# First loads split over two queues, angles started from the second: the opening of a fused pooling and attention layer

## The chip, the cores and the metric

The kernel runs on one core of one Trainium2 chip. The metric is the device time of one execution in microseconds; the median of several executions counts.

## The reference, cut to what matters

One layer on x of 256 tokens by 1024 channels, all in float32: one projection gives six parts, a pooling branch and an attention branch are computed from them, each is multiplied by SiLU of its gate, one output projection follows, then a residual and a layer norm.

```python
proj = jnp.einsum('bsd,de->bse', h, w_in[layer])
u_pool, g_pool, q, k, v, g_attn = jnp.split(proj, cuts, axis=-1)
y_pool = multiscale_pool(u_pool, pool_w[layer], pool_scale[layer]) * jax.nn.silu(g_pool)
q = partial_rotary(q.reshape(b, s, N_HEADS, HEAD_DIM), positions)
k = partial_rotary(k.reshape(b, s, N_HEADS, HEAD_DIM), positions)
y_attn = moba_attention(q, k, v) * jax.nn.silu(g_attn)
out = jnp.einsum('bse,ed->bsd', jnp.concatenate([y_pool, y_attn], axis=-1), w_out[layer])
h = layer_norm(ALPHA * h + out, ln_gain[layer], ln_bias[layer])

def partial_rotary(x, positions):        # the angles that this change moves
    ang = positions.astype(jnp.float32)[..., None] * freqs
    cos, sin = jnp.cos(ang)[:, :, None, :], jnp.sin(ang)[:, :, None, :]
    ...
```

With 256 tokens there is one key block, so attention is causal attention over all keys.

## The kernel before, in words

Every float32 matmul is done as three fast ones: an operand is split into a high part (a cast to fp32r, `hi`, line 307) and a low part (what the cast lost, a subtraction, `lo`, line 318), and high x high, low x high and high x low are added up in PSUM. ScalarE makes the casts (its rows have line 310), VectorE or GpSimd the subtractions (line 320).

The first stage is the value projection v (lines 430 to 462). The inner dimension of 1024 is cut into eight blocks k = 0 to 7 of 128. A block is one row of `xw`: 256 columns of x, transposed, and 512 columns of value weights, 384 KB together. `load_xw` (line 325) loads it, block 0 in two pieces (512 columns, then 256), the others in one. ScalarE casts x and the weights of a block; of block 0 the weights are cast by VectorE in two halves (line 312). VectorE subtracts. TensorE then runs six matmuls of 512 columns a block (line 454; eight in block 0, where the first two are halved): high x times high weights, low x times high weights, high x times low weights.

Behind it come twenty units of 128 output columns, in the order u0 u1 q0 k0 q1 k1 and so on. A unit has its own 512 KB of weights: one load (`load_w`, line 331), one cast by ScalarE, one or two subtractions, 24 matmuls of 256 columns (lines 501 to 503, in two halves of twelve). Rotary embedding (`rope`), scores, softmax, the pooling windows and the gates are interleaved, then the output projection (lines 770 to 772) and the norm follow.

The angles of the rotary embedding have a path of their own. The positions and a small tensor of constants are loaded (`posi`, line 337, and `cst`, line 338). GpSimd multiplies them and reduces the angles to the range of the sine in a chain of small instructions (lines 348 to 377). ScalarE takes two sines (lines 388 and 389), GpSimd makes the cosines (lines 394 and 395), TensorE transposes both (line 526), and ScalarE copies them out (line 529) for `rope`.

TensorE begins with warm-up matmuls on a constant (`warm`, line 297), ScalarE with the load of its function table (line 288).

The order of the instructions on each engine is no list in the source. `add` collects operations with costs by engine; `Plan.run` simulates them, picks on every engine the operation that can start first (among equals the one that is due first), and emits the code in the order of the simulated starts. A constant in the plan can therefore move instructions. Loads are emitted by the plan's engine "SP" whichever queue they go to. A load needs a free slot of `raw` (seven of them), given back by the subtraction that reads it.

Of the kernel before, what the change touches and what calls it, by code (L numbers as in the profile page):

```python
# [63 lines left out]
class Op:  # L64
    __slots__ = ("i", "options", "emit", "bufs", "deps", "outs", "late", "left", "ready", "start", "end", "eng", "pos", "port")


class Plan:
# [4 lines left out]
    MARGIN = 1.0  # L73

# [3 lines left out]
    def add(self, options, emit, reads=(), writes=(), pos=None, port=False):  # L78
        op = Op()
        op.port = port  # L80
# [24 lines left out]
    def run(self, pools, limits, dma_rate=0.34, ahead=3):  # L105
# [5 lines left out]
        for op in reversed(ops):  # L111
            cost = min(c for c in op.options.values())
# [27 lines left out]
        while n < len(ops):  # L140
            best = None
            for e in free:
# [19 lines left out]
                elif e == "SP":  # L162
                    at, op = min(cand, key=lambda c: (c[1].late, c[1].i))
# [58 lines left out]
def hymba_kernel(ctx: ExitStack, tc: tile.TileContext, xw, xn, pos, small_in, w, wo, pw, ln, out):  # L222
# [42 lines left out]
    cst = const.tile([P, RD + 4 + 4 * PAD], F32, name="cst")  # L265
    frq = cst[:, :RD]
    pscale = cst[:, RD:RD + 4]
    fac = cst[:, RD + 4:].rearrange("p (g t) -> p g t", g=4)
    posi = const.tile([P, 2], I32, name="posi")
# [18 lines left out]
    act.preload_act_table_set("trig_and_small")  # L288
# [12 lines left out]
    add({"PE": 3.0}, warm, writes=[wb], pos=at())  # L301


    def load(dst, src, mb, writes):
        add({"SP": mb}, lambda e: nc.sync.dma_start(dst(), src), writes=writes)  # L305

    def hi(dst, src, n, reads, writes, fast=False):
# [5 lines left out]
        options = c_act(n)  # L313
        if fast:
            options["DVE"] = 0.18 + n * 0.00055
        add(options, emit, reads, writes)
# [31 lines left out]
    tiny(lambda e: pool.tensor_copy(posf, posi), ["posi"], ["posf"])  # L348
# [30 lines left out]
    add({"POOL": 3.5}, reduction, [("ang", 0), ("ang", 1)], ["ang"], port=None)  # L379
# [51 lines left out]
    for k in range(KT):  # L431
# [7 lines left out]
        if k == 0:  # L439
            for h in range(2):  # L440
                hi(lambda wH=wH, c=c, h=h: wH[:, c + h * S:c + h * S + S], lambda r=r, h=h: r[:, S + h * S:2 * S + h * S],
                   S, [(r, 1 + h)], [kh(u, k, h)], fast=True)
# [454 lines left out]
```

## Time and profile before

| | us |
|---|---|
| median of 3 runs | 118.07 (117.93 to 118.69) |
| the profiled execution | 118.58 |
| its span in the profile | 116.8 |
| TensorE busy in the span | 108.7 |
| VectorE, ScalarE, GpSimd busy | 81.7, 66.7, 45.8 |

The profile is one execution. Its times start at the first instruction of the span; 1.78 us of the execution lie around the span. PE is TensorE's matmuls, PEld its weight loads, DVE VectorE, ACT ScalarE, POOL GpSimd, SP SyncE; a q behind a name is the engine's sequencer, which issues DMAs and waits. The starts of matmuls are measured, their ends are modelled: a matmul shows longer than it keeps the next one away.

### The profile page before, as it was taken

The page shows a single profiled execution, that of the slowest core. Times are in us where ns is not written, and L with a number is a line of the kernel's source. Part 1 is how long each engine was busy: PE and PEld are TensorE (multiplying, and loading weights), DVE is VectorE, ACT ScalarE, POOL GpSimd, SP SyncE. Part 2 cuts the span into 40 slices and gives each one's busy share as a digit, 9 for nine tenths or more (in the row PEclk, how much of TensorE's full clock was granted, in tenths as well). Part 3 has the DMA queues.
Part 4 walks back from the last instruction along what each step waited for, and adds up shares of the span by engine and source line. Part 5 has one row for each costly group of instructions (what it writes and reads, how often), then busy time and mean ns, then how long its engine had stood idle before and what let it go on. Part 6 is the DMA issues. An engine that isn't in the chain of part 4 may idle for free.

```text
span 116.8 us, 2214 instructions
## 1 busy us (share of the span) xinstructions
PE 108.7 (93%) x809; PEld 98.6 (84%) x809; DVE 81.7 (70%) x182; ACT 66.7 (57%) x132; POOL 45.8 (39%) x66
## 2 busy tenths in 40 slices
PE   7998999999999999999999999999999999999800
PEld 5745889999998999988999898899998989789700
DVE  0539972189999987987868576498897933942780
ACT  4149770599837698598888665524669800120510
POOL 7200687500192689979777320000612600053000
PEclk9999999999999999999999999999999999999997
DMA  3999999929999894596757082500000000022013
GB/s 112 285 349 371 392 384 415 384 108 269 323 316 349 282 349 187 126 412 279 236 205 268 17 264 95 180 6 0 0 0 0 3 6 0 0 90 90 0 54 128
DMA packets 6779, 21.42 MB, mean 183 GB/s; under 512 B 1008, under 2 KB 1520, under 8 KB 6512
## 3 DMA queue, kind: packets, MB, share of 16 engines
q1 hardware_dynamic: 6624, 21.08, 50.7%
q10 hardware_dynamic: 144, 0.20, 0.5%
q8 instruction: 6, 0.10, 0.3%
q14 instruction: 5, 0.04, 0.1%
HBM read 20.23 MB, written 1.05 MB: 182 GB/s over the span
## 4 chain that ended last, share of the span: by engine, by line
PE 60%; DVE 10%; POOL 7%; issue 6%; DMA 6%; ACT 4%; SPq 3%; DVEq 0%; ACTq 0%
PE acc L501 12%; PE acc L502 11%; PE acc L503 11%; DMA posi<-pos 6%; DVE w L320 4%; SPq L305 3%; PE acc L771 3%; PE acc L772 3%; PE acc L770 3%; PE sc L554 3%; PE tp L589 3%; PE sc L771 2%; PE sc L772 2%; PE sc L770 2%; POOL tb L357 2%
## 5 line engine op out<-in xcount | busy, mean ns | idle before, releaser
L501 PE MATMUL acc<-big,w 128*128 128x256 f32 x160 | 45.8, 286 | 0.0
L503 PE MATMUL acc<-big,w 128*128 128x256 f32 x160 | 44.9, 281 | 0.0
L502 PE MATMUL acc<-big,w 128*128 128x256 f32 x160 | 44.8, 280 | 0.0
L320 DVE TENSOR_TENSOR w<-raw,w 128x1024 fp32r<-128x1024 f32 (+1 forms) x31 | 31.2, 1024 | 12.9 <-ACT w L310 11.3
L501 PEld LDWEIGHTS acc<-big,w 128*128 128x128 f32 x160 | 30.2, 189 | 0.7 <-issue 0.5
L502 PEld LDWEIGHTS acc<-big,w 128*128 128x128 f32 x160 | 30.2, 188 | 0.0
L503 PEld LDWEIGHTS acc<-big,w 128*128 128x128 f32 x160 | 30.1, 188 | 0.1
L310 ACT CAST w<-raw 128x1024 fp32r<-128x1024 f32 (+1 forms) x27 | 24.8, 941 | 6.9 <-DMA raw<-xw 3.7
L320 POOL TENSOR_TENSOR w<-raw,w 128x1024 fp32r<-128x1024 f32 x5 | 13.1, 2618 | 12.0 <-ACT w L310 12.0
L454 PE MATMUL acc<-w,big 128*128 128x512 f32 (+1 forms) x50 | 13.4, 419 | 0.8 <-ACT big L310 0.7
L454 PEld LDWEIGHTS acc<-w,big 128*128 128x128 f32 x50 | 9.6, 210 | 4.4 <-ACT big L310 1.9
L579 POOL TENSOR_SCALAR pr<-pr,rv 128x256 f32<-128x256 f32 (+1 forms) x16 | 10.6, 680 | 3.1 <-DVE rv L576 3.1
L475 ACT ACTIVATE w<-raw 128x1024 fp32r<-128x1024 f32 x6 | 6.4, 1061 | 6.9 <-issue 5.0
L320 POOL TENSOR_TENSOR mL<-m,mH 128x256 fp32r<-128x256 f32 x2 | 1.7, 871 | 16.9 <-ACT mH L310 16.9
L573 ACT ACTIVATE pr<-ms,mx 128x256 f32<-128x256 f32 (+1 forms) x16 | 7.1, 448 | 1.1 <-DVE mx L568 1.0
L807 POOL TENSOR_TENSOR xnat<-xnat,gb 128x512 f32<-128x512 f32 x2 | 2.6, 1288 | 11.1 <-ACT xnat L805 11.1
L771 PE MATMUL acc<-w,mH 128*128 128x256 f32 (+1 forms) x18 | 5.7, 319 | 0.0
L772 PE MATMUL acc<-w,mL 128*128 128x256 f32 (+1 forms) x18 | 5.7, 319 | 0.0
L770 PE MATMUL acc<-w,mH 128*128 128x256 f32 (+1 forms) x18 | 5.7, 318 | 0.0
L568 DVE CUSTOM_DVE_ANT_0 ms<-sc,mask 128x256 f32<-128x256 f32 (+1 forms) x16 | 4.8, 347 | 0.8 <-PE sc L554 0.8
L801 ACT ACTIVATE rs<-mv,epst 128x1 f32<-128x1 f32 x1 | 0.3, 295 | 8.5 <-DVE mv L800 8.5
L538 DVE TENSOR_TENSOR qk<-t,t 128x512 f32<-128x512 f32 x4 | 5.1, 1270 | 0.0
(153 smaller groups left out, 195.2 us busy)
## 6 DMA issues: line engine op xcount, KB each, us to landing
raw<-w SPq DMA_DIRECT2D x20, 512.0 KB, 5.4
raw<-wo SPq DMA_DIRECT2D x8, 512.0 KB, 3.5
raw<-xw SPq DMA_DIRECT2D x7, 384.0 KB, 6.7
xnat<-xn SPq DMA_DIRECT2D x1, 1024.0 KB, 7.5
gb<-ln SPq DMA_DIRECT2D x1, 1024.0 KB, 6.2
out<-xnat SPq DMA_DIRECT2D x2, 256.0 KB, 2.0
raw<-xw SPq DMA_DIRECT2D x1, 256.0 KB, 2.7
raw<-pw SPq DMA_DIRECT2D x1, 256.0 KB, 3.3
```

The costliest lines, as they stand in the source:

```text
L310: act.copy(dst(), src())
L320: lambda e: engines[e].tensor_tensor(dst(), raw(), h().bitcast(F32), op=OP.subtract), reads, writes, port=True)
L454: pe.matmul(vb[s][:, o:o + n], x(k, s * P, P), b[:, c + o:c + o + n], start=first and o == 0, stop=last)
L475: act.activation(wH[:, :D], r[:], AF.Identity, accum_out=ws[:])
L501: pe.matmul(o[:, half], wH[:, c], xh(k, 0, S), start=k == 0, stop=False)
L502: pe.matmul(o[:, half], wH[:, c], xl(k, 0, S), start=False, stop=False)
L503: pe.matmul(o[:, half], wL[:, c], xh(k, 0, S), start=False, stop=k == KT - 1)
L573: add(c_act(n, 0.28), lambda e, t=t, sl=sl: act.activation(pr[:, sl], ms[:, sl], AF.Exp, bias=mx[:, t:t + 1], scale=-1.0, accum_out=sm[:, ...
L579: add({"POOL": 0.25 + 0.00105 * n}, lambda e, t=t, sl=sl: pool.tensor_scalar(pr[:, sl], pr[:, sl], rv[:, t:t + 1], 0.5, op0=OP.mult, op1=O ...
L770: pe.matmul(o[:, :n], mH[:, e, sl], wH[:, c0:c0 + n], start=i == 0, stop=False)
L771: pe.matmul(o[:, :n], mH[:, e, sl], wL[:, c0:c0 + n], start=False, stop=False)
L772: pe.matmul(o[:, :n], mL[:, e, sl], wH[:, c0:c0 + n], start=False, stop=i == 7)
```

## The change

Six edits, all at the start of the program:

- Block 0 of x is loaded in other pieces: the 256 columns of x by SyncE's queue, the 512 columns of value weights by ScalarE's queue.
- Positions and constants become one tensor (344 instead of 336 bytes a partition), loaded by ScalarE's queue right behind those weights. SyncE loads only blocks of x and weights there. Loads of the start carry a fixed rank (`pos`).
- The load of ScalarE's function table becomes an operation of the plan, behind its two DMA issues.
- 16 warm-ups instead of 15.
- Both halves of the weights of block 0 are cast by VectorE in both kernels; what was offered as a choice is now fixed.
- The plan counts some things longer: the angles 6.2 instead of 3.5 us, ScalarE busy for 0.9 us at the start, matmuls at the start slower (`COLD`), the constants 2.8 us later.

```diff
+    ISSUE = 0.9
+    COLD = 5.2
...
+        free["ACT"] = self.ISSUE
...
-                    at, op = min(cand, key=lambda c: (c[1].late, c[1].i))
+                    at, op = min(cand, key=lambda c: (c[1].late if c[1].pos is None else c[1].pos, c[1].i))
...
+            if e == "PE" and op.deps and at < self.COLD:
+                cost += min(cost, (self.COLD - at) / 2)
...
-                op.end = dma + 0.5
+                op.end = dma + 0.5 + op.tail
...
-    posi = const.tile([P, 2], I32, name="posi")
+    posi = cst[:, RD + 4 + 4 * PAD:].bitcast(I32)
...
-    act.preload_act_table_set("trig_and_small")
...
-        for _ in range(15):
+        for _ in range(16):
...
-        for a, b in ((0, 512), (512, 768)) if k == 0 else ((0, 768),):
+        for a, b, queue in ((0, S, nc.sync), (S, 768, act)) if k == 0 else ((0, 768, nc.sync),):
...
     load_xw(0)
-    load_xw(1)
-    add({"SP": 0.02}, lambda e: nc.sync.dma_start(posi, pos), writes=["posi"])
-    add({"SP": 0.04}, lambda e: nc.sync.dma_start(cst, small_in), writes=["cst"])
-    for k in range(2, KT):
+    add({"SP": 0.04}, lambda e: act.dma_start(cst, small_in), writes=["cst"], pos=-98.1, tail=2.8)
+    add({"ACT": 1.3}, lambda e: act.preload_act_table_set("trig_and_small"))
+    for k in range(1, KT):
         load_xw(k)
...
-    tiny(lambda e: pool.tensor_copy(posf, posi), ["posi"], ["posf"])
+    tiny(lambda e: pool.tensor_copy(posf, posi), ["cst"], ["posf"])
...
-    add({"POOL": 3.5}, reduction, [("ang", 0), ("ang", 1)], ["ang"], port=None)
+    add({"POOL": 6.2}, reduction, [("ang", 0), ("ang", 1)], ["ang"], port=None)
```

TensorE's order stays as it is but for the 16th warm-up, and so does GpSimd's. SyncE's list loses its second load, the positions and the constants: it is now one load of 128x256, seven of 128x768 and the units' weights. ScalarE and VectorE have another order in the first 25 us. In the changed kernel line 309 issues the loads that line 305 issued, 314 and 316 are the casts of lines 310 and 312, 321 is the subtraction of line 320. `raw` takes a load, `big` holds the split x, `w` split weights.

ScalarE's list before, from its start:

```order
L893 UNCONDITIONAL_BRANCH
L288 ACT_TABLE_LOAD
L310 CAST big<-raw 128x256
L310 CAST w<-raw 128x512
L310 CAST big<-raw 128x256
```

And now:

```order
L894 UNCONDITIONAL_BRANCH
L309 DMA raw<-xw 128x512
L337 DMA cst<-small 128x86
L338 ACT_TABLE_LOAD
L314 CAST big<-raw 128x256
L314 CAST w<-raw 128x512
```

Two DMA issues moved in front of the table load; the casts behind it are the same.

ScalarE's list before, around the sines (`tb` and `csrc` take the sines, `vn` the finished v; a cast of 128x1024 is that of a unit):

```order
L310 CAST big<-raw 128x256
L310 CAST w<-raw 128x1024 x2
L388 ACTIVATE tb<-ang 128x32
L389 ACTIVATE csrc<-ang 128x2x32
L310 CAST w<-raw 128x1024
L462 COPY vn<-acc 128x512
L310 CAST w<-raw 128x1024
L462 COPY vn<-acc 128x512
```

And now:

```order
L314 CAST big<-raw 128x256
L314 CAST w<-raw 128x1024
L388 ACTIVATE tb<-ang 128x32
L389 ACTIVATE csrc<-ang 128x2x32
L314 CAST w<-raw 128x1024
L462 COPY vn<-acc 128x512
L314 CAST w<-raw 128x1024 x2
L462 COPY vn<-acc 128x512
```

The sines moved ahead of the second unit's cast, the first copy of v ahead of the third's.

VectorE's list before, from its start:

```order
L893 UNCONDITIONAL_BRANCH
L312 CAST w<-raw 128x256 x2
L320 TENSOR_TENSOR big<-raw,big 128x256
L320 TENSOR_TENSOR w<-raw,w 128x512 x2
L320 TENSOR_TENSOR big<-raw,big 128x256
```

And now:

```order
L894 UNCONDITIONAL_BRANCH
L321 TENSOR_TENSOR big<-raw,big 128x256
L316 CAST w<-raw 128x256 x2
L321 TENSOR_TENSOR w<-raw,w 128x512 x2
L321 TENSOR_TENSOR big<-raw,big 128x256
```

The low part of x (`big<-raw,big`), which needs ScalarE's cast, moved ahead of both weight casts of block 0.

## Rows read from the trace of the kernel before

**Rows 1.** The profile's page: the span, TensorE's busy time with its share of the span and its instructions, and the shares of the chain that ended last, by engine.

```profile
span 116.8 us, 2214 instructions
PE 108.7 (93%) x809; PEld 98.6 (84%) x809; DVE 81.7 (70%) x182; ACT 66.7 (57%) x132; POOL 45.8 (39%) x66
...
PE 60%; DVE 10%; POOL 7%; issue 6%; DMA 6%; ACT 4%; SPq 3%; DVEq 0%; ACTq 0%
```

**Rows 2.** The windows view: a stretch, its length, busy time of PE, PEld, DVE, ACT and POOL (instructions in brackets), granted clock, DMA share, GB/s.

```profile
4.00:9.25 5.25, 4.48 (x15) 2.90 (x15) 2.33 (x6) 1.85 (x4) 0.00 (x0) 1.00 0.97 345
9.25:18.00 8.75, 8.72 (x37) 6.82 (x38) 8.01 (x16) 6.74 (x12) 4.75 (x11) 1.00 1.01 386
18.00:36.70 18.70, 18.70 (x160) 18.65 (x159) 13.48 (x17) 11.94 (x17) 7.00 (x16) 1.00 0.85 303
...
110.20:116.80 6.60, 0.21 (x2) 0.01 (x1) 3.12 (x10) 0.29 (x1) 0.00 (x0) 0.89 0.23 81
```

**Rows 3.** The waits of TensorE's weight loads over the whole span: who waited for whom, us in total, times, longest.

```profile
PEld acc L454 <- ACT big L310: 1.9, 3, 1.0
PEld acc L454 <- DVE big L320: 0.9, 2, 0.5
...
PEld sc L554 <- DVE qkl L320: 0.3, 1, 0.3
```

**Rows 4.** The timeline of TensorE's weight loads, 3 to 19 us: start, us, what, and in brackets the idle time before it and what ended that. Six (in block 0 eight) belong to a block.

```profile
6.72 0.30 PEld L454 LDWEIGHTS acc<-w,big 128*128 128x128 f32 x2 [0.60 <-ACT big L310]
7.48 0.76 PEld L454 LDWEIGHTS acc<-w,big 128*128 128x128 f32 x4 [0.46 <-DVE big L320]
9.25 0.30 PEld L454 LDWEIGHTS acc<-w,big 128*128 128x128 f32 x2 [1.01 <-ACT big L310]
10.00 7.70 PEld L454 LDWEIGHTS acc<-w,big 128*128 128x128 f32 x34 [0.46 <-DVE big L320]
```

**Rows 5.** The timeline of ScalarE, 0 to 24 us, with the casts of blocks 0, 1, 2 and 7 and of the first unit.

```profile
3.44 0.40 ACT L310 CAST big<-raw 128x256 fp32r<-128x256 f32 x1 [1.42 <-DMA raw<-xw]
5.75 0.62 ACT L310 CAST w<-raw 128x512 fp32r<-128x512 f32 x1 [1.91 <-DMA raw<-xw]
...
8.27 0.62 ACT L310 CAST w<-raw 128x512 fp32r<-128x512 f32 x1 [1.60 <-DMA raw<-xw]
...
13.34 0.62 ACT L310 CAST w<-raw 128x512 fp32r<-128x512 f32 x1 [0.22 <-DMA raw<-xw]
...
14.62 1.05 ACT L310 CAST w<-raw 128x1024 fp32r<-128x1024 f32 x1 [0.35 <-DMA raw<-w]
...
21.67 0.23 ACT L388 ACTIVATE tb<-ang 128x32 f32<-128x32 f32 x1 [4.73 <-POOL ang L377]
...
21.95 1.03 ACT L310 CAST w<-raw 128x1024 fp32r<-128x1024 f32 x1
```

**Rows 6.** The timeline of GpSimd, 3 to 23 us: the first, the twelfth and the last of the 22 instructions of the angles.

```profile
12.44 0.19 POOL L348 CAST posf<-posi 128x2 f32<-128x2 int32 x1 [8.79 <-DMA posi<-pos]
...
18.35 0.25 POOL L367 TENSOR_TENSOR ta<-ta,tb 128x32 f32<-128x32 f32 x1
...
21.42 0.21 POOL L377 TENSOR_SCALAR ang<-ang 128x32 f32<-128x32 f32 x1
```

**Rows 7.** The timeline of VectorE, 3 to 26 us: block 0, and the subtraction for q0.

```profile
3.44 0.60 DVE L312 CAST w<-raw 128x256 fp32r<-128x256 f32 x2 [3.44 <-DMA raw<-xw]
3.95 0.42 DVE L320 TENSOR_TENSOR big<-raw,big 128x256 fp32r<-128x256 f32 x1
4.29 0.69 DVE L320 TENSOR_TENSOR w<-raw,w 128x512 fp32r<-128x512 f32 x1
...
23.02 1.23 DVE L320 TENSOR_TENSOR w<-raw,w 128x1024 fp32r<-128x1024 f32 x1 [4.74 <-ACT w L310]
```

**Rows 8.** The timeline of TensorE's matmuls, 23.9 to 24.6 us: the first matmuls of q0.

```profile
23.97 0.37 PE L501 MATMUL acc<-big,w 128*128 128x256 f32 x1
...
24.52 0.28 PE L501 MATMUL acc<-big,w 128*128 128x256 f32 x1
```

**Rows 9.** The timeline of TensorE's matmuls, 0 to 19 us: the warm-ups, block 0, and the first matmul of u0.

```profile
0.78 3.36 PE L299 MATMUL pv<-const-float32-0.0 128*128 128x256 bf16 x15 [0.78 <-PEq L890]
3.94 2.61 PE L454 MATMUL acc<-w,big 128*128 128x256 f32 x8
...
17.98 0.28 PE L501 MATMUL acc<-big,w 128*128 128x256 f32 x1
```

**Rows 10.** The DMA view: what, queue, count, KB each, median us from issue to landing.

```profile
raw<-xw SPq DMA_DIRECT2D x1, 256.0 KB, 2.7
...
cst<-small SPq DMA_DIRECT2D x1, 42.0 KB, 6.7
```

**Rows 11.** The instructions of line 849, its DMA issue on ScalarE: count, ns least/median/most, start.

```profile
L849 ACTq DMA_DIRECT2D out<-raw x1: 376/376/376, 113.1 to 113.1; - x1
```

**Rows 12.** The timeline of ScalarE, 36 to 42 us: its second table load and the instruction behind it.

```profile
37.29 1.28 ACT L573 ACT_TABLE_LOAD   x1
39.61 0.51 ACT L573 ACTIVATE pr<-ms,mx 128x256 f32<-128x256 f32 x1 [1.04 <-DVE mx L568]
```

**Rows 13.** The timeline of SyncE's DMA issues, 0 to 117 us: the first eight, of blocks 0 to 6, and that of the constants.

```profile
0.74 4.33 SPq L305 DMA_DIRECT2D raw<-xw  x8
...
5.90 0.60 SPq L338 DMA_DIRECT2D cst<-small  x1
```

More of the change, by code (lines that the diff above doesn't have):

```diff
@@ L64 @@
 class Op:
-    __slots__ = ("i", "options", "emit", "bufs", "deps", "outs", "late", "left", "ready", "start", "end", "eng", "pos", "port")
+    __slots__ = ("i", "options", "emit", "bufs", "deps", "outs", "late", "left", "ready", "start", "end", "eng", "pos", "port", "tail")
 class Plan:
@@ L73, with add @@
     MARGIN = 1.0
+    ISSUE = 0.9
+    COLD = 5.2
     def __init__(self):
         self.ops, self.writer, self.readers, self.n_pe = [], {}, {}, 0
-    def add(self, options, emit, reads=(), writes=(), pos=None, port=False):
+    def add(self, options, emit, reads=(), writes=(), pos=None, port=False, tail=0.0):
         op = Op()
-        op.port = port
+        op.port, op.tail = port, tail
         op.i, op.options, op.emit, op.pos = len(self.ops), options, emit, pos
@@ L111, in run @@
         for op in reversed(ops):
-            cost = min(c for c in op.options.values())
+            cost = min(op.options.values()) + op.tail
             late = min((o.late for o in op.outs), default=1e3) - cost
@@ L221, in hymba_kernel @@
 @with_exitstack
-def hymba_kernel(ctx: ExitStack, tc: tile.TileContext, xw, xn, pos, small_in, w, wo, pw, ln, out):
+def hymba_kernel(ctx: ExitStack, tc: tile.TileContext, xw, xn, small_in, w, wo, pw, ln, out):
     nc = tc.nc
@@ L263, in xl @@
         return xbig[1][:, k * S + a:k * S + a + n]
-    cst = const.tile([P, RD + 4 + 4 * PAD], F32, name="cst")
+    cst = const.tile([P, RD + 4 + 4 * PAD + 2], F32, name="cst")
     frq = cst[:, :RD]
     pscale = cst[:, RD:RD + 4]
-    fac = cst[:, RD + 4:].rearrange("p (g t) -> p g t", g=4)
-    posi = const.tile([P, 2], I32, name="posi")
+    fac = cst[:, RD + 4:RD + 4 + 4 * PAD].rearrange("p (g t) -> p g t", g=4)
+    posi = cst[:, RD + 4 + 4 * PAD:].bitcast(I32)
     posf = const.tile([P, 2], F32, name="posf")
@@ L297, in warm, with load, hi @@
     def warm(e):
-        for _ in range(15):
+        for _ in range(16):
             pe.matmul(wb[:, :S], wz.to_broadcast([P, P]), wz.to_broadcast([P, S]), start=True, stop=True)
[L301 to L307, printed above, removed]
+    add({"PE": 3.35}, warm, writes=[wb], pos=at())
+    def load(dst, src, mb, writes, queue=nc.sync, pos=None):
+        add({"SP": mb}, lambda e: queue.dma_start(dst(), src), writes=writes, pos=pos)
+    def hi(dst, src, n, reads, writes, only=None):
         def emit(e):
@@ L312, in emit @@
                 dve.tensor_copy(dst(), src())
[L313 to L316, printed above, removed]
+        add({"DVE": 0.18 + n * 0.00055} if only == "DVE" else c_act(n), emit, reads, writes)
     def lo(dst, raw, h, n, reads, writes, options=None):
@@ L326, in load_xw @@
         raw["x", k] = r = Buf("raw", [P, D])
-        for a, b in ((0, 512), (512, 768)) if k == 0 else ((0, 768),):
+        for a, b, queue in ((0, S, nc.sync), (S, 768, act)) if k == 0 else ((0, 768, nc.sync),):
             load(lambda r=r, a=a, b=b: r[:, a:b], xw[k, :, a:b], (b - a) * 0.000512,
-                 [(r, c) for c in range(a // 256, b // 256)])
+                 [(r, c) for c in range(a // 256, b // 256)], queue, k + a / D - 99)
     def load_w(u):
@@ L441, in hymba_kernel @@
                 hi(lambda wH=wH, c=c, h=h: wH[:, c + h * S:c + h * S + S], lambda r=r, h=h: r[:, S + h * S:2 * S + h * S],
[L442 removed]
+                   S, [(r, 1 + h)], [kh(u, k, h)], "DVE")
         else:
@@ L878 @@
     f = (np.float32(THETA) ** (-np.arange(HALF, dtype=np.float32) * np.float32(2.0) / np.float32(16.0))).astype(np.float32)
-    small = np.zeros((P, RD + 4 + 4 * PAD), np.float32)
+    small = np.zeros((P, RD + 4 + 4 * PAD + 2), np.float32)
     small[:, :HALF] = f
@@ L884 @@
         small[:, RD + 4 + g * PAD:RD + 4 + (g + 1) * PAD] = wn / np.minimum(np.arange(PAD) + 1.0, wn)
+    small[:, RD + 4 + 4 * PAD:] = np.ascontiguousarray(np.asarray(positions).reshape(2, P).T).view(np.float32)
     arrays = {
-        "xw": xw, "xn": xn, "pos": np.ascontiguousarray(np.asarray(positions).reshape(2, P).T), "small": small,
+        "xw": xw, "xn": xn, "small": small,
         "w": wall, "wo": wo, "pw": pw,
```

## The prediction

> **What bounds the kernel now.** Read first the page's busy table and chain [rows 1]: TensorE is busy 108.7 of 116.8 us and holds 60% of the chain, so the end is set by when TensorE gets through its list. The cut into stages comes second [rows 2]: from 9.25 to 18.00 it is busy 8.72 of 8.75 us, from 18.00 to 36.70 all of it, and the 6.6 us behind 110.2 are a tail that starts when TensorE stops. Time can come only from when its list becomes dense and from holes in it. The holes are in the waits of its weight loads [rows 3]: 1.9 us for ScalarE's casts of x, 0.9 us for VectorE's low part of x, 0.3 us for qkl. The timeline of the same loads [rows 4] places the first five: block 1 waits 0.60 at 6.72 and 0.46 at 7.48, block 2 waits 1.01 at 9.25 and 0.46 at 10.00; from there nothing. So blocks 0 to 2 of the value projection are starved, and ScalarE's timeline says by what [rows 5]: each of its casts at 3.44, 5.75 and 8.27 ended a wait for the load of x. Transfers bound the first 9 us.
>
> A second wait hides behind TensorE. ScalarE stands 4.73 us before the sines at 21.67, because the angles start at 12.44, when the positions land [rows 5, 6]. Behind the sines stand its casts of the next weights; VectorE's subtraction for q0 starts at 23.02 after 4.74 idle and ends at 24.25 [rows 7], just when TensorE wants it: the three matmuls from 23.97 take 0.55 us to 24.52 [rows 8], against 0.35 at the 0.117 that one takes in the stage 18.00 to 36.70 (18.70 us, 160 matmuls). The idle time is also missing later, when qkl is late.
>
> The sums go against the profiled execution, 118.58 us: span 116.8 and 1.78 around it. The median of the runs is 118.07 (117.93 to 118.69), so the profiled one is among the later.
>
> **Block 0.** A 16th warm-up adds 0.21 us (fifteen in 3.36, rows 9), so they end near 4.15 instead of 3.94. The first 128 KB of x now travel alone on SyncE's queue and the 256 KB of value weights on ScalarE's. Bounds for x: in the trace 256 KB are there at 3.44, by ScalarE's wait [rows 5], and the 128 KB behind them before VectorE's second cast, which ended at 4.04 and took some 0.3, so by 3.75 [rows 7]. If the queues share evenly, x is there at 3.75, with all 384 KB; if x goes ahead, at about 2.9 (an estimate: half of the bytes that needed 2.7 us, rows 10). I take 3.3. ScalarE issues two DMAs first, 0.38 each by its one issue in the trace [rows 11], against nothing before, so its table load of 1.28 us runs from 1.6 to 2.9. How soon a cast can follow it is bounded by the second table load: the next instruction began 2.32 us after its start, and that one was waiting for VectorE [rows 12]. So the first cast starts between 2.9 and 3.93; I take 3.5, near the landing.
>
> [...]
>
> Then a chain: cast 0.40; on VectorE the low part of x now stands ahead of both weight casts (the two VectorE lists), 0.34 from its start to the next start (3.95 to 4.29, rows 7); weight cast 0.36. 3.5 + 0.40 + 0.05 + 0.34 + 0.31 gives the first real matmul at 4.6 (bounds 4.15 and 5.05) where it was 3.94. Behind the low part of x both casts and all of VectorE wait. [...]
>
> **Blocks 1 and 2.** Block 1's load is now second on SyncE's queue instead of third, issued some 0.5 us earlier (eight issues in 4.33 us, rows 13), but 43 KB of constants now travel ahead of its end: at 345 GB/s [rows 2] 0.12 us. So it lands between 0.5 earlier and 0.12 later than 5.75; I take 5.5. [...]
>
> [...] This trace has no two loads on different queues at once. [...]
>
> Block 2 decides. It landed at 8.27, 2.52 after block 1, while blocks 2 to 7 came on average within 1.01 of each other (8.27 to 13.34, rows 5). Its bounds are 6.5 (block 1 plus that pace) and 8.4 (as before plus the constants). The trace does not say why it was late; between ends that each have a row I take the middle, 7.45, because the profiled execution is 0.5 above the median. Block 2 then starts at 7.45 + 0.98 = 8.43 instead of 9.25: **0.8 us gained**, bounds 0.1 lost and 1.0 gained, plus up to 0.4 if TensorE no longer runs into the low part at 10.00. Blocks 3 to 7 are TensorE's own pace, so the issues of positions and constants that block 7 stood behind on SyncE (0.60 for the second, rows 13) gain nothing there. SyncE's load of block 6 now waits for ScalarE's first load to land, by 3.8; in the trace its issue, the eighth, ran until 5.07, so nothing behind it is pushed back.
>
> **Angles.** The constants were issued at 5.90 and landed 6.7 later [rows 13, 10]; now ScalarE issues them near 1.15. They land between 3.75 (with block 0) and 7.9 (6.7 again); I take 5.8, with block 1. From 12.44 GpSimd needed 9.2 us to 21.64, of which eleven instructions took 5.9 beside a VectorE busy for 8.01 of 8.75 us, and the other eleven 3.3 beside one that idles until 23.02 [rows 6, 2, 7]; beside a busy one all would take 11.8. With 11 the angles are ready at 16.8. ScalarE gets to the sines at 15.67, after the first weight cast (14.62 + 1.05), and waits 1.1. Queued behind is the cast of u1, which used to stand ahead of the sines (ScalarE's lists around the sines), then VectorE's subtraction of it, then TensorE, which wants u1 at 20.0 (17.98 - 0.8 + 2.81). Sines 0.28, cast 1.0, subtraction 0.8: ready 2.1 after the angles, 18.9, so the cover is 1.1. After that a copy of v and the cast of q0 run near 19, three microseconds before 21.95; the hole at 24 (0.2) and the 0.3 for qkl go: **0.5 us gained**, bounds 0.2 and 0.6. With the cover gone every further microsecond is lost whole.
>
> All later orders are the same, so nothing else is charged. Sum: 118.58 - 0.8 - 0.5 = **117.3**, 0.8 under the median.
>
> **The rivals.**
> - Loads as late as before: block 2 starts at 9.25 whatever the queues do, only the angles gain. For it: the wait at 8.27 is the transfer's, and the bytes are the same. 118.58 - 0.5 = 118.1.
> - Loads at pace: block 2 at 8.25, no wait for the low part: 118.58 - 1.0 - 0.4 - 0.5 = 116.7. For it: five blocks in the trace came at 1.01.
> - Slower: the angles are late for u1. The constants, alone behind 256 KB on ScalarE's queue, take turns with SyncE's stream and land at 7.9; beside a busy VectorE the reduction ends at 19.7, u1 is ready at 21.8 instead of 20.8 (17.98 + 2.81), whatever the first blocks gained: +1.0, and only some 0.4 comes back later. 119.2; later still, microsecond for microsecond. It decides from angles ready after 17.9. Against it: they start over 4 us earlier than before.
> [...]
>
> [...]
>
> **How the numbers follow.** Forecast 0.35; loads as before 0.23; loads at pace 0.18; angles late 0.12; clock late 0.12. Within 1% of the median is 116.9 to 119.25, about what a measurement of this kernel can tell from no change. Faster by more: most of the pace case (0.15) and a fifth of the forecast (0.07). Slower by more: half of the late angles (0.06), and the clock case with late loads or a longer idle (0.06). The range leaves out the best of the pace case and the worse half of late angles: 116.4 to 118.8.
>
> **What would show it.** Right: the first real matmul at 4.2 to 5.1 with VectorE's low part of x ahead of it; block 2's weight load before 8.8; angles ready by 17.9; the weight loads' wait for qkl gone; the stage behind 38 us as long as before. Wrong: block 2 at 9.2 or later, 0.21 per 256 columns beyond 6.5 us, or a wait on the first matmuls of u1.

## The result and the profile after

The changed kernel took **116.88 us** (median of 9 runs, 116.70 to 117.22), the kernel before 117.87 beside it (9 runs, 117.36 to 118.69): a ratio of **0.990**, interval 0.988 to 0.993. Measured again in another series, it took 117.01 against 118.35, 0.989 (0.985 to 0.992). It is faster by about 1%; the median lies 0.4 us below the 117.3 that was forecast. A ratio leaves out single executions that took over 1.5% longer than the fastest of their kernel; medians have all of them. The profiled execution took 117.12, against 118.58 for the one before, so this pair of profiles shows 1.5 us where the medians show 1.0 and 1.3.

The page of the changed kernel, with the rows that answer to [rows 1]:

```profile
span 115.3 us, 2215 instructions
...
PE 107.6 (93%) x810; PEld 97.7 (85%) x810; DVE 83.2 (72%) x182; ACT 67.2 (58%) x132; POOL 45.8 (40%) x66
...
PE 85%; DMA 5%; DVE 3%; ACT 3%; SPq 1%; DVEq 0%; issue 0%
```

TensorE is busy 1.1 us less with one matmul more, and holds 85% of the chain instead of 60%. The weight loads' waits over the whole span [rows 3], the first two rows:

```profile
PEld acc L454 <- ACT big L314: 2.0, 3, 0.9
PEld acc L454 <- DVE big L321: 0.9, 2, 0.5
```

The wait for qkl is gone from the list. The waits for the first blocks are as long as before in sum, so they have to be read by their places, in the timeline of the weight loads [rows 4]:

```profile
4.79 1.25 PEld L454 LDWEIGHTS acc<-w,big 128*128 128x128 f32 x8 [0.92 <-ACT big L314]
6.39 0.30 PEld L454 LDWEIGHTS acc<-w,big 128*128 128x128 f32 x2 [0.35 <-ACT big L314]
7.15 0.76 PEld L454 LDWEIGHTS acc<-w,big 128*128 128x128 f32 x4 [0.46 <-DVE big L321]
8.62 0.30 PEld L454 LDWEIGHTS acc<-w,big 128*128 128x128 f32 x2 [0.72 <-ACT big L314]
9.39 7.71 PEld L454 LDWEIGHTS acc<-w,big 128*128 128x128 f32 x34 [0.47 <-DVE big L321]
```

Block 0 begins later and is through sooner; block 1 is ready 0.33 us earlier than before (6.39 for 6.72), block 2 0.63 earlier (8.62 for 9.25), and from 9.39 the list is dense. TensorE's matmuls [rows 9] say the same:

```profile
0.77 3.57 PE L303 MATMUL pv<-const-float32-0.0 128*128 128x256 bf16 x16 [0.77 <-PEq L891]
4.82 3.52 PE L454 MATMUL acc<-w,big 128*128 128x256 f32 x14 [0.47 <-DVE w L316]
...
17.38 0.28 PE L501 MATMUL acc<-big,w 128*128 128x256 f32 x1
```

u0 begins at 17.38 instead of 17.98: 0.60 us. The other 0.9 of the 1.5 us between the two profiled executions lie behind it. They show in the rows of the scores (line 554) and of the output projection (line 772): count, ns least, median and most, first and last start. The scores of the kernel before:

```profile
L554 PE MATMUL sc<-qkh x16: 322/326/331, 37.0 to 60.6; 64*128 64x128 f32 x8, 64*128 64x256 f32 x8
```

And of the changed one:

```profile
L554 PE MATMUL sc<-qkh x16: 323/326/331, 36.2 to 59.4; 64*128 64x128 f32 x8, 64*128 64x256 f32 x8
```

The last matmuls of line 772, before:

```profile
L772 PE MATMUL tp<-big,mL x2: 282/283/284, 109.8 to 110.1; 128*128 128x256 f32 x2
```

And now:

```profile
L772 PE MATMUL tp<-big,mL x2: 282/284/285, 108.6 to 108.9; 128*128 128x256 f32 x2
```

The scores start 0.8 us earlier, the last matmul of line 772 1.2, and the span ends 1.5 earlier. So 0.6 came from the opening, 0.2 between u0 and the scores, 0.4 between the scores and the last matmul (0.3 of it the wait for qkl, as its row in [rows 3] has it) and 0.3 after it. ScalarE's timeline [rows 5] shows what became of the two steps:

```profile
1.17 0.46 ACTq L337 DMA_DIRECT2D cst<-small  x1
1.65 1.28 ACT L338 ACT_TABLE_LOAD   x1 [1.65 <-PEq L891]
3.60 0.40 ACT L314 CAST big<-raw 128x256 fp32r<-128x256 f32 x1 [0.67 <-DMA raw<-xw]
5.41 0.62 ACT L314 CAST w<-raw 128x512 fp32r<-128x512 f32 x1 [1.40 <-DMA raw<-xw]
...
7.64 0.62 ACT L314 CAST w<-raw 128x512 fp32r<-128x512 f32 x1 [1.31 <-DMA raw<-xw]
...
15.74 0.23 ACT L388 ACTIVATE tb<-ang 128x32 f32<-128x32 f32 x1 [0.90 <-POOL ang L377]
```

The casts of blocks 0, 1 and 2 still end a wait for a load, now at 3.60, 5.41 and 7.64. The sines come at 15.74 instead of 21.67, after a wait of 0.90 instead of 4.73. GpSimd's first and last instruction of the angles [rows 6] say why:

```profile
5.63 0.18 POOL L348 CAST posf<-cst 128x2 f32<-128x2 int32 x1 [1.99 <-DMA cst<-small]
...
15.17 0.54 POOL L377 TENSOR_SCALAR ang<-ang 128x32 f32<-128x32 f32 x1
```

And in the DMA view [rows 10] the loads of block 0 and the constants, with KB and the median us from issue to landing:

```profile
raw<-xw ACTq DMA_DIRECT2D x1, 256.0 KB, 3.0
...
raw<-xw SPq DMA_DIRECT2D x1, 128.0 KB, 2.8
...
cst<-small ACTq DMA_DIRECT2D x1, 43.0 KB, 4.4
```

The constants land 4.4 us after their issue at 1.17, GpSimd starts at 5.63 instead of 12.44, and its chain of angles takes 10.1 us to 15.7, where it took 9.2; VectorE is busy beside it for 7.9 of the 10.1 us, against 5.1 of the 9.2 before. VectorE now subtracts with a stop of 0.53 us where it had stood for 4.74 [rows 7] (that its four subtractions in the row also take 4.74 is chance):

```profile
4.04 0.43 DVE L321 TENSOR_TENSOR big<-raw,big 128x256 fp32r<-128x256 f32 x1 [4.04 <-ACT big L314]
...
18.91 4.74 DVE L321 TENSOR_TENSOR w<-raw,w 128x1024 fp32r<-128x1024 f32 x4 [0.53 <-ACT w L314]
```

### The profile page after: what moved, and what is told of

Same layout as the page of the kernel before. It is cut to its first block, busy times and chain, and to the rows that moved or that the text cites. A ratio compares the mean times of both kernels' runs of the same rounds, so it can differ in the third digit from the quotient of the medians.

```text
span 115.3 us, 2215 instructions
## 1 busy us (share of the span) xinstructions
PE 107.6 (93%) x810; PEld 97.7 (85%) x810; DVE 83.2 (72%) x182; ACT 67.2 (58%) x132; POOL 45.8 (40%) x66
## 3 DMA queue, kind: packets, MB, share of 16 engines
HBM read 20.23 MB, written 1.05 MB: 184 GB/s over the span
## 4 chain that ended last, share of the span: by engine, by line
PE 85%; DMA 5%; DVE 3%; ACT 3%; SPq 1%; DVEq 0%; issue 0%
PE acc L501 17%; PE acc L502 16%; PE acc L503 16%; PE acc L454 8%; DMA raw<-xw 5%; PE acc L771 3%; PE acc L772 3%; PE acc L770 3%; PE sc L554 3%; PE tp L589 3%; PE sc L771 2%; PE sc L772 2%; PE sc L770 2%; PE pv L603 2%; ACT raw L830 1%; DVE raw L846 1%
## 5 line engine op out<-in xcount | busy, mean ns | idle before, releaser
L321 POOL TENSOR_TENSOR w<-raw,w 128x1024 fp32r<-128x1024 f32 x5 | 11.9, 2396 | 16.9 <-ACT w L314 16.9
L454 PE MATMUL acc<-w,big 128*128 128x512 f32 (+1 forms) x50 | 12.4, 395 | 0.8 <-DVE w L316 0.5
L454 PEld LDWEIGHTS acc<-w,big 128*128 128x128 f32 x50 | 8.8, 188 | 4.5 <-ACT big L314 2.0
L321 DVE TENSOR_TENSOR big<-raw,big 128x256 fp32r<-128x256 f32 (+1 forms) x9 | 4.8, 528 | 4.0 <-ACT big L314 4.0
L538 DVE TENSOR_TENSOR qk<-t,t 128x512 f32<-128x512 f32 x4 | 5.6, 1400 | 0.0
```

Of the source, the lines that this page charges most:

```text
L321: lambda e: engines[e].tensor_tensor(dst(), raw(), h().bitcast(F32), op=OP.subtract), reads, writes, port=True)
L454: pe.matmul(vb[s][:, o:o + n], x(k, s * P, P), b[:, c + o:c + o + n], start=first and o == 0, stop=last)
```

## The experiments

Theory: two gains that add up, one in the opening (block 2 is there earlier) and one behind it (the angles no longer hold ScalarE and VectorE back). Rivals: only the angles gain; only the opening gains; the pace of TensorE's matmuls decides. There are two paces, read from the starts of the matmuls: in the changed kernel 256 columns take 0.21 us in the warm-ups and 0.12 behind u0 (160 matmuls in the 18.60 us from 17.40), while the granted clock reads 1.00 in both stretches. The expectations call the paces a low and a high level of the clock and the step between them its rise; no run shows that it is the clock that changes. Each diff below is against the changed kernel. Every run left a profile of one execution, and these are their times from the timelines of TensorE: first matmul of blocks 0, 1 and 2 and of u0, the execution, and what lies between u0 and its end.

| kernel | block 0 | block 1 | block 2 | u0 | execution | from u0 on |
|---|---|---|---|---|---|---|
| before | 3.94 | 6.72 | 9.25 | 17.98 | 118.58 | 100.60 |
| changed | 4.82 | 6.39 | 8.62 | 17.38 | 117.12 | 99.74 |
| changed, again | 4.66 | 6.15 | 8.73 | 17.49 | 117.22 | 99.73 |
| angles alone | 4.12 | 7.16 | 8.96 | 17.51 | 117.37 | 99.86 |
| loads alone | 4.91 | 7.60 | 10.16 | 18.51 | 118.22 | 99.71 |
| weights cast first | 4.26 | 6.35 | 8.75 | 17.49 | 117.20 | 99.71 |
| VectorE casts blocks 1, 2 | 4.73 | 6.23 | 7.66 | 16.20 | 116.03 | 99.83 |
| angles late, order kept | 4.53 | 6.04 | 8.70 | 17.42 | 119.35 | 101.93 |
| 12 warm-ups | 4.77 | 7.46 | 9.03 | 17.35 | 117.08 | 99.73 |
| one queue | 4.46 | 6.87 | 8.44 | 16.77 | 116.58 | 99.81 |
| both orders of casts | 4.20 | 6.22 | 7.95 | 16.43 | 116.23 | 99.80 |
| 20 warm-ups | 4.85 | 6.46 | 8.31 | 17.12 | 116.85 | 99.73 |
| both and 20 warm-ups | 4.85 | 6.52 | 8.23 | 16.74 | 116.53 | 99.79 |
| blocks exchanged | 4.75 | 6.61 | 8.47 | 17.23 | 116.98 | 99.75 |

The last column is the most useful one here: 99.7 to 99.9 in all twelve profiles in which the angles are in time, 100.60 before, 101.93 where they are late. The part behind u0 hardly moves; the opening is what differs from one execution to the next.

**Angles alone.** The loads of block 0 and the warm-ups as before.

```diff
-        for _ in range(16):
+        for _ in range(15):
...
-        for a, b, queue in ((0, S, nc.sync), (S, 768, act)) if k == 0 else ((0, 768, nc.sync),):
+        for a, b, queue in ((0, 512, nc.sync), (512, 768, nc.sync)) if k == 0 else ((0, 768, nc.sync),):
```

> Only the angles part: positions and constants in one tensor on ScalarE's queue, sines ahead of u1's cast; block 0 is loaded as before (512 and 256 columns by SyncE), 15 warm-ups, weight casts ahead of x's low part. Theory A (two gains that add: 0.5 from the first blocks, 0.5 from the angles): 117.4, block 2's weights begin at 9.0 to 9.3, no hole at q0, no wait for qkl. Rival B (the gain is all in the first blocks): 117.9, as before. Rival C (the gain is all in the angles): 116.9.

Measured: 117.33 us, ratio 0.993 (0.989 to 0.996). Some two thirds of the gain are there with the angles alone: 0.86 us (0.73% of 118.23), near the 0.74 by which its last column is below that of before. But its opening was shorter too: u0 at 17.51, 0.47 earlier than before, though block 0 was loaded in the old pieces on one queue. Nearly as much as the changed kernel's 0.60 was thus there in one profile without the split loads.

**Loads alone.** Constants on SyncE's queue behind block 6, the sines where the kernel before had them.

```diff
-    add({"SP": 0.04}, lambda e: act.dma_start(cst, small_in), writes=["cst"], pos=-98.1, tail=2.8)
+    add({"SP": 0.04}, lambda e: nc.sync.dma_start(cst, small_in), writes=["cst"], pos=6.9 - 99)
...
-    add({"POOL": 6.2}, reduction, [("ang", 0), ("ang", 1)], ["ang"], port=None)
+    add({"POOL": 3.5}, reduction, [("ang", 0), ("ang", 1)], ["ang"], port=None)
```

> Only the loads part: block 0 split over both queues, 16 warm-ups, x's low part first; the constants stay on SyncE's queue behind block 6, the sines behind u1's cast as before. Theory A: 117.4, block 2 at 8.6, all 0.5 kept to the end. Rival B: 116.9. Rival D (the gains do not add: with late angles q0's weights are ready at 24.2 whatever TensorE does, so what the first blocks gain is given back there): 117.8, block 2 at 8.6 and a wait of some 0.5 us of TensorE's loads at q0 near 23.5.

Measured: 117.24 us, ratio 0.991 (0.988 to 0.994), as good as the whole change. That looks as if the angles gained nothing, but the profile says otherwise. ScalarE's first sine:

```profile
20.30 0.23 ACT L388 ACTIVATE tb<-ang 128x32 f32<-128x32 f32 x1 [4.73 <-POOL ang L377]
```

ScalarE still waits 4.73 us, but at 20.30 instead of 21.67, since the constants stand two issues nearer to the front of SyncE's queue. That is enough: no wait before q0, none for qkl, and 99.71 in the last column, so rival D, that the gain is given back at q0, did not occur. (Before, the subtraction for q0 ended 2.58 us behind the start of the sines [rows 5, 7], which here makes 22.9 by estimate; q0 is wanted 6.0 us behind u0 [rows 8, 9], which even with a u0 at 17.4 is 23.4.) This part of the change brings the angles forward by 1.4 us by itself, so the two experiments share a gain, and their ratios must not be added. Its profiled execution had the worst opening of all. TensorE's timeline:

```profile
4.91 13.77 PE L454 MATMUL acc<-w,big 128*128 128x256 f32 x50 [0.56 <-DVE w L316]
18.51 0.28 PE L501 MATMUL acc<-big,w 128*128 128x256 f32 x1
```

The value projection takes 13.6 us from 4.91 to 18.51 without one wait between its matmuls; block 0 and block 1 need 2.7 and 2.6 us in the table, 0.22 and 0.21 per 256 columns (a block has twelve times 256), where the six matmuls of a block take 1.4 in the changed kernel from 9.73 on (33 starts in the 7.65 us to u0). u0 came 1.1 us later than in the changed kernel, although block 2 had landed 1.1 us sooner (ScalarE's cast at 6.51 for 7.64).

**Weights cast first.** VectorE makes the weight casts of block 0 ahead of the low part of x, as before.

```diff
-           [(r, 0), (xbig[0], k)], [(xbig[1], k)])
+           [(r, 0), (xbig[0], k)] + ([kh(u, 0, 0), kh(u, 0, 1)] if k == 0 else []), [(xbig[1], k)])
```

> The changed kernel with VectorE's two weight casts of block 0 ahead of x's low part again. Theory A (block 0 is not on the path, block 1's load is): first real matmul 0.3 earlier, at 4.5, block 1 at 6.4 and block 2 at 8.6 as now, 116.9. Rival E (the later first matmul costs its 0.3): 116.6.

Measured: 117.03 us, ratio 0.988 (0.984 to 0.993): no difference from the changed kernel that can be told. Block 0 starts at 4.26, 0.56 earlier, and block 2 at 8.75, no earlier. In this profile the start of block 0 is off the path; the 0.3 us of rival E would lie within the interval of the times.

**VectorE casts blocks 1 and 2 as well.** ScalarE then casts only their x.

```diff
-        if k == 0:
+        if k <= 2:
```

> The changed kernel with the weights of blocks 1 and 2 cast by VectorE too, while ScalarE casts only their x. Theory A (what counts is block 2's landing plus the casts behind it): a block is usable 0.65 after it lands instead of 0.98 and the wait for x's low part, 0.47 in each of the two blocks, shrinks; block 2 at 8.25, u0 at 16.7 instead of 17.4, 116.2 to 116.4. Rival F (something behind the first blocks binds by now, u0's own load or the casts of the units): u0 or u1 waits and the time stays at 116.9.

Measured: 116.80 us (6 runs), 0.988 of the median before; the ratio of 0.984 (0.978 to 0.989) rests on four of them and leaves out 117.67 and 118.27. That this kernel is faster than the changed one is not shown. The weight loads of its profile, with all waits in the first eight blocks:

```profile
4.70 2.66 PEld L454 LDWEIGHTS acc<-w,big 128*128 128x128 f32 x14 [0.90 <-ACT big L314]
7.63 2.16 PEld L454 LDWEIGHTS acc<-w,big 128*128 128x128 f32 x10 [0.28 <-ACT big L314]
10.04 5.89 PEld L454 LDWEIGHTS acc<-w,big 128*128 128x128 f32 x26 [0.25 <-DVE w L321]
```

The two waits of 0.46 for the low part of x are gone: one cast of 0.4 stands between a landing and the low part, not one of 0.5 and one of 0.4. u0 starts at 16.20, the earliest of all, with the shortest waits. Part of that is the load: block 2 landed at 6.97 there, 0.65 sooner than in the changed kernel (7.62). ScalarE stood 2.13 us at the sines there, and nothing behind u0 was late.

**Angles late, the new order kept.** The constants go back to SyncE's queue, but the sines stay ahead of the cast of u1.

```diff
-    add({"SP": 0.04}, lambda e: act.dma_start(cst, small_in), writes=["cst"], pos=-98.1, tail=2.8)
+    add({"SP": 0.04}, lambda e: nc.sync.dma_start(cst, small_in), writes=["cst"], pos=6.9 - 99, tail=-3.5)
```

> The changed kernel with the constants loaded late, by SyncE behind block 6 (they landed at 11.0 there), while the sines stay ahead of u1's cast on ScalarE. Theory A with the price of the lost cover: angles ready near 20.3, u1's weights 2.1 later at 22.4 instead of some 20.0, so TensorE waits for u1 about 2 us and q0 gives nothing back: 118.6 to 119.2. Rival (u1's cast is not needed that early, or the wait is made up by later slack): 116.9 to 117.3.

Measured: 119.24 us, ratio 1.012 (1.005 to 1.018): slower than before. ScalarE's first sine in its profile:

```profile
20.40 0.23 ACT L388 ACTIVATE tb<-ang 128x32 f32<-128x32 f32 x1 [5.32 <-POOL ang L377]
```

TensorE in the second half of u1:

```profile
20.11 0.28 PE L503 MATMUL acc<-big,w 128*128 128x256 f32 x1
21.76 0.39 PE L501 MATMUL acc<-big,w 128*128 128x256 f32 x1 [1.37 <-ACT w L314]
...
22.49 0.39 PE L503 MATMUL acc<-big,w 128*128 128x256 f32 x1 [0.22 <-DVE w L321]
```

u1 was wanted at 20.23 and waited for ScalarE's cast, then for VectorE's subtraction. From u0 on this kernel takes 2.19 us more than the changed one, and none of it is given back. This is the slower rival of the prediction, at its place and at its price.

**12 warm-ups.**

```diff
-        for _ in range(16):
+        for _ in range(12):
```

> The changed kernel with 12 warm-ups instead of 16, so that TensorE idles from 3.3 to 4.8 us instead of 4.15 to 4.8. Theory G (the time at which the clock rises has nothing to do with this idle time; it differed between executions by itself, 3.7 to 10.2 us in the profiles so far): the median stays at 116.9, with the same spread. Rival H (the idle time ahead of block 0 delays the rise): most executions run blocks 0 and 1 at the low level, 117.5 to 118.

Measured: 117.60 us (12 runs), ratio 0.997 (0.994 to 1.000), against 0.990 and 0.989 with 16, in intervals that do not meet: some 0.8 us lost. The changed kernel itself was not run in that series, though, nor beside the next two kernels, which belong to it; an offset of the whole series is not ruled out (both orders of casts gave 0.989 in it and, with 20 warm-ups, 0.984 in another). The one profiled execution, among the fastest, does not show that loss; what it shows is a slow block 0. The matmuls of block 0 by line: count, busy us, mean ns of one (ends are modelled, so the means serve for comparison). The kernel before:

```profile
L454 PE MATMUL acc<-w,big 128*128 128x256 f32 (+1 forms) x8 | 2.6, 497 | 0.0
```

The changed kernel:

```profile
L454 PE MATMUL acc<-w,big 128*128 128x256 f32 (+1 forms) x8 | 1.6, 348 | 0.5 <-DVE w L316 0.5
```

The kernel with 12 warm-ups:

```profile
L454 PE MATMUL acc<-w,big 128*128 128x256 f32 (+1 forms) x8 | 2.9, 538 | 1.3 <-DVE w L316 1.3
```

The same eight matmuls take 2.6, 1.6 and 2.9 us, that is 0.22, 0.13 and 0.24 per 256 columns: near the slow pace, near the fast one, and near the slow one again after TensorE had idled 1.3 us between the warm-ups and block 0. That the idle time did it is not shown: the kernel with the loads alone had as slow a block 0 (2.7) behind 16 warm-ups and 0.6 us.

**One queue.** Both pieces of block 0 on SyncE's queue.

```diff
-        for a, b, queue in ((0, S, nc.sync), (S, 768, act)) if k == 0 else ((0, 768, nc.sync),):
+        for a, b, queue in ((0, S, nc.sync), (S, 768, nc.sync)) if k == 0 else ((0, 768, nc.sync),):
```

> The changed kernel with both pieces of block 0 on SyncE's queue (128 KB of x, then 256 KB of weights); only the constants go by ScalarE's. Theory I (the second queue gives block 1 and 2 an earlier issue, and that is the loads' gain): block 1 lands near 5.9, block 2 near 7.9, u0 begins 0.3 to 0.5 later, 117.2. Rival J (the gain comes from anything but the queue: the pieces, or the constants off SyncE's list): 116.9.

Measured: 117.47 us (12 runs), ratio 0.994 (0.991 to 0.997), against 0.990 and 0.989 for the changed kernel: the second queue seems worth some 0.5 us, but the intervals overlap and come from different series. Where it is gained stays open, for the profiled execution was the fastest of the twelve. ScalarE's first rows in it:

```profile
3.10 0.40 ACT L314 CAST big<-raw 128x256 fp32r<-128x256 f32 x1 [0.64 <-DMA raw<-xw]
5.61 0.62 ACT L314 CAST w<-raw 128x512 fp32r<-128x512 f32 x1 [2.11 <-DMA raw<-xw]
...
6.84 0.62 ACT L314 CAST w<-raw 128x512 fp32r<-128x512 f32 x1 [0.30 <-DMA raw<-xw]
```

x in front of the queue is cast at 3.10, half a microsecond sooner than with two queues, and block 2, at 6.84, came 1.2 us behind block 1.

**Both orders of casts**, that is weights first in block 0 and VectorE's casts of blocks 1 and 2:

```diff
-        if k == 0:
+        if k <= 2:
...
-           [(r, 0), (xbig[0], k)], [(xbig[1], k)])
+           [(r, 0), (xbig[0], k)] + ([kh(u, 0, 0), kh(u, 0, 1)] if k == 0 else []), [(xbig[1], k)])
```

> The changed kernel with VectorE's casts ahead of x's low part in block 0 and VectorE casting the weights of blocks 1 and 2 as well. Theory A: as with the casts of blocks 1 and 2 alone, 1.0 us under the changed kernel where block 2 lands by 7.0 and some 0.5 where it lands at 7.7: 116.2 to 116.6; the earlier block 0 adds nothing. Rival E: a further 0.3 from block 0, 116.0.

Measured: 116.45 us, ratio 0.989 (0.984 to 0.993). The opening of its profile is short again (u0 at 16.43), but the ratio does not repeat the 0.984 of VectorE's casts alone: the two intervals overlap, and a difference from the changed kernel is not shown.

**20 warm-ups**, and the same with both orders of casts, beside the changed kernel:

```diff
-        for _ in range(16):
+        for _ in range(20):
```

> The changed kernel with 20 warm-up matmuls instead of 16; nothing else differs. 16 of them end at 4.3 us, and the first real matmul waits until 4.8; four more at 0.21 would run to 5.2, so they fill that idle time and push block 0 back by some 0.4, where a wait for block 1 follows it anyway. Theory A (the idle time ahead of block 0 is part of what lets TensorE's clock rise late in some executions): the rise comes earlier on the whole, median 116.3 to 116.7, ratio to the kernel before 0.983 to 0.988. Theory B (the moment of the rise does not hang on so short an idle time; block 2's landing sets the stream): the same as the changed kernel, 116.8 to 117.2, 0.988 to 0.993, with block 0 0.4 later and block 2 where it was. Twelve warm-ups gave 0.9967.

> The kernel with VectorE's weight casts of block 0 ahead of its low part of x and the weight casts of blocks 1 and 2 on VectorE too (0.9886 [0.9841, 0.9931] with 16 warm-ups), now with 20 warm-ups. Theory A (a fuller TensorE before block 0 brings the clock up sooner): 116.0 to 116.4, ratio 0.979 to 0.984. Theory B (the warm-ups above 16 do nothing, and the casts are worth what they were): 116.4 to 116.9, 0.984 to 0.990. Block 0 starts at about 5.2 instead of 4.2 by either, and blocks 1 to 3 at 6.3 to 9.4 as before.

> The changed kernel itself, beside the two kernels with 20 warm-ups, so that all three have the same runs of the kernel before next to them. Expected 0.988 to 0.993 of the kernel before, as in its first runs (0.9902 [0.9876, 0.9928]). If it comes out below 0.986 or above 0.995, differences of 0.5% between kernels of different calls say nothing here.

Measured side by side: 20 warm-ups 116.80 us, ratio 0.988 (0.985 to 0.992); the changed kernel 117.01, 0.989 (0.985 to 0.992); both orders and 20 warm-ups **116.38 us** (116.15 to 116.53), 0.984 (0.981 to 0.987). Beyond 16, warm-ups alone do nothing that can be told here. The last is the best version of the study, 0.5% under the changed kernel by the medians, though the lowest run of the changed kernel (116.34) lies among its own and the intervals overlap; what in it belongs to the casts and what to the warm-ups is not separated. Its weight loads:

```profile
4.78 2.84 PEld L454 LDWEIGHTS acc<-w,big 128*128 128x128 f32 x14
8.20 0.76 PEld L454 LDWEIGHTS acc<-w,big 128*128 128x128 f32 x4 [0.57 <-ACT big L314]
9.11 1.24 PEld L454 LDWEIGHTS acc<-w,big 128*128 128x128 f32 x6 [0.16 <-DVE w L321]
10.57 5.89 PEld L454 LDWEIGHTS acc<-w,big 128*128 128x128 f32 x26 [0.22 <-DVE w L321]
```

Block 1 starts without a wait, and the four waits that the changed kernel had behind block 0, 2.00 us, have become three of 0.95.

**Blocks exchanged.** Blocks 2 and 4 of x and the value weights change places in the order of loading and of use.

```diff
+PERM = [0, 1, 4, 3, 2, 5, 6, 7]
...
-            load(lambda r=r, a=a, b=b: r[:, a:b], xw[k, :, a:b], (b - a) * 0.000512,
+            load(lambda r=r, a=a, b=b: r[:, a:b], xw[PERM[k], :, a:b], (b - a) * 0.000512,
```

> The changed kernel with blocks 2 and 4 of x and the value weights exchanged in their order of loading and of use; the output is not affected. In both traces the load of block 2, the third on SyncE's queue, came 2.2 to 2.5 us behind block 1, against 1.0 a block on average. Theory A (it is its place in the queue, or what the other queue carries at that time): block 4, now third, comes 1.5 to 2.5 us behind block 1 as well, ScalarE's third cast starts at 6.7 to 8.3, and the value weights of block 2 come later without a gap. Theory B (it is that block's place in memory): the third load is there 1.0 to 1.3 us behind block 1, and the fifth is late. The other executions so far had the third load between 6.5 and 8.25, so a single look weighs little if it falls between.

ScalarE's casts of the second and the third load in it:

```profile
4.89 0.62 ACT L316 CAST w<-raw 128x512 fp32r<-128x512 f32 x1 [0.95 <-DMA raw<-xw]
...
7.50 0.62 ACT L316 CAST w<-raw 128x512 fp32r<-128x512 f32 x1 [1.68 <-DMA raw<-xw]
```

The third load came 2.6 us behind the second again, though it was another block. That speaks for its place in the queue and against its place in memory; as a single execution (116.98 us) of something that varies it does not settle it.

The traces say more of what is late. They hold sixteen landing signals for each load, and the cast that waits for it starts just behind the last (for block 2 at 8.27 behind 8.25 before, at 7.64 behind 7.62 in the changed kernel). When fifteen of block 2's had come, and when the last came, in us:

| kernel | fifteenth | last | last behind |
|---|---|---|---|
| before | 6.99 | 8.25 | 1.26 |
| changed | 6.82 | 7.62 | 0.80 |
| changed, again | 7.12 | 7.73 | 0.61 |
| angles alone | 7.62 | 7.73 | 0.11 |
| one queue | 6.75 | 6.81 | 0.06 |
| blocks exchanged (block 4) | 6.64 | 7.47 | 0.83 |

In three of these six the last signal comes 0.8 us or more behind the other fifteen, and the cast of block 2 waits for it alone. Why it is late, and by so different a time, stays open.

## Why the prediction came out right, step by step

The time was within the range and near the sum (117.3 for the profiled execution, which took 117.12), and the path that it named held: the first blocks wait for their loads, and late angles hold up ScalarE and VectorE. But the two terms were mis-sized in opposite directions: the opening gave 0.6 of the 0.8 forecast, the angles and what lies behind them 0.9 of the 0.5. That the sum came out within 0.2 us is in part luck.

- **Block 0.** Forecast 4.6, measured 4.82, within its bounds. x did not go ahead of its weights: issued together, the 128 KB took 2.8 us and the 256 KB 3.0, so x was there at some 3.55 and not at 3.3. The bound "if the queues share evenly" was the nearer one; the other, 2.9, does not follow from the half that it names (half of 2.7 us behind an issue at 0.74 is 2.1). The start did not matter (weights cast first: 0.56 earlier, nothing gained).
- **The table load** adds no delay. The first cast starts 1.95 us after the load's start (1.65 to 3.60) and its wait is for x. The second load of the table in the changed kernel settles what [rows 12] left open:

```profile
36.05 1.28 ACT L573 ACT_TABLE_LOAD   x1
37.70 0.51 ACT L573 ACTIVATE pr<-ms,mx 128x256 f32<-128x256 f32 x1 [0.36 <-DVE mx L568]
```

The next instruction starts 1.65 us after the load's start, and had still waited for VectorE, so that beyond the 1.28 of the load at most 0.37 can be its own.

- **Block 1.** Landing 5.5 forecast, 5.41 measured; usable 0.98 behind that, at 6.39. TensorE was done with block 0 before, since from the second matmul on it ran at 0.12 us per 256 columns (the starts from 5.03 to 6.07), and so the 0.46 wait for the low part of x stayed, at no cost: block 2 came later.
- **Block 2.** Landing 7.45, measured 7.64; start 8.43, measured 8.62. The 7.45 was the middle between two ends and named no cause, so that it came within 0.2 is luck: block 2 landed between 6.49 (loads alone) and 8.25 (before) in the profiles. Of the 0.63 us by which it landed earlier than before, 0.17 are in its fifteenth signal; the rest is how late the last one was, which also differs between two executions of the changed kernel (0.80 and 0.61). How much of the gain here the new loads made is not shown.
- **The angles.** Constants 5.8, measured 5.6 (1.17 and 4.4); angles 16.8, measured 15.7, since the chain took 10.1 us and not 11; ScalarE's wait 1.1, measured 0.90. The limit of 17.9 was tested by the experiment with late angles: u0 at 17.42 puts it at 18.1, the angles were ready at 20.36, and 2.19 us were lost. The working was right to 0.1 us.
- **Behind u0.** Of the term of 0.5 (hole at q0 0.2, qkl 0.3) the 0.3 was there, by the rows above. The hole gave 0.11: the three matmuls that took 0.55 us before [rows 8] still take 0.44, the first of them 0.20 in both kernels:

```profile
23.37 0.37 PE L501 MATMUL acc<-big,w 128*128 128x256 f32 x1
...
23.81 0.28 PE L501 MATMUL acc<-big,w 128*128 128x256 f32 x1
```

What the term missed are 0.2 in the rest of the list and 0.3 between the last matmul and the end. That 0.3 lies with the last output transfer: ScalarE issues its part at 112.0 of 115.3 now (111.95 in its timeline), and at 113.1 of 116.8 before [rows 11]. From the start of TensorE's last matmul to the end of the span it is 6.67 us before, 6.41 now and 6.38 to 6.53 in all other profiles. Of the kernel before there is one profile only, so whether the longer end is its own or that execution's stays open.

By the ratios the split is somewhat more one-sided. Angles alone give 0.86 us; the whole change gave 1.2 and 1.35 (0.98% of 117.87, 1.14% of 118.35). The opening adds 0.3 to 0.5, which no experiment resolves well: the intervals are 0.6 to 0.9 us wide. The reason is in the table: block 2 starts between 7.66 and 10.16, and u0 between 16.2 and 18.5, with small edits that in part do not touch it. Two things move it from one execution to the next. One is block 2's load, whose cast waited until 8.27 before, 7.64 in the changed kernel and 6.84 with one queue. The other is the moment at which TensorE leaves the slow pace: block 0 took 1.6 us in the changed kernel, 2.4 with one queue and 2.7 with the loads alone, behind the same 16 warm-ups. What sets either moment is not settled, and the 0.8 us of fewer warm-ups is not tied to it.

**Rivals.** Loads as late as before did not occur: block 2 started at 8.62 and 8.73 in the changed kernel's two profiles, not at 9.25. But with block 0 loaded as before it started at 8.96 (angles alone), so that most of this is the work of the queues is not shown. Loads at pace did not occur in the changed kernel; the run with one queue came near to it. Late angles are real, 2.2 us, and the change stays clear of them by 2.4 us (15.7 against 18.1). The chances have a term for a late clock; no run shows it, the granted clock reading 1.00 at either pace. What the runs showed in its place is the slow pace through blocks 0 and 1 in the run with the loads alone (0.22 and 0.21 us per 256 columns), whose u0 came 1.1 us later than in the changed kernel.

## What to carry over

Cut the time of an execution at the first instruction from which the bound engine is dense: here what lies behind that point was the same to 0.15 us in twelve profiles, and what lies ahead of it differed by over 2 us between profiles of kernels that load the same bytes, so that a gain in the opening needs medians and one behind it a single profile. When a dependent chain on other engines (load, small operations, table function) is moved ahead of casts that the bound engine needs, work out the limit at which it starts to hold them up; it was met to 0.1 us here. Casts shared out so that only one stands between a landing and the next step are what to try next: in the profiles they shortened the waits that the order of the loads had left, though by the times alone a gain over the changed kernel is not yet clear.

## What the runs showed of the hardware that was not expected

- Two loads issued at the same time on two queues, 128 and 256 KB, landed 2.8 and 3.0 us later: the small one gained almost nothing from its own queue. In front of the weights on one queue it took 2.3 us from issue, by that kernel's DMA view:

```profile
raw<-xw SPq DMA_DIRECT2D x1, 128.0 KB, 2.3
```

- Block 2's load came 1.2 us (one queue, casts at 5.61 and 6.84) to 2.9 us (weights first, casts at 4.92 and 7.78) behind block 1's, the ones behind it about 1.0 apart, and late also with another block in its place. Between 0.06 and 1.26 us of that is the lag of the last of its sixteen landing signals, in the kernels of the table of signals.
- Behind 16 warm-ups TensorE ran its first block at 0.22 us per 256 columns in one execution (loads alone) and at 0.12 from the second matmul on in another (the changed kernel), while the granted clock column read 1.00 for both; only the spacing of matmuls shows it. The windows view in the first blocks with the loads alone (2.7 us for block 0):

```profile
6.00:8.00 2.00, 2.00 (x6) 1.55 (x6) 1.76 (x4) 1.16 (x4) 0.00 (x0) 1.00 1.00 378
```

And in block 0 of the changed kernel (1.6):

```profile
4.80:6.30 1.50, 1.49 (x8) 1.15 (x8) 1.00 (x3) 0.89 (x2) 0.56 (x3) 1.00 0.91 292
```
